# Scores of mixer A from rounded high and low parts of the keys, and a weight pool of 16 tiles of 4 KB

## The chip, the cores and the metric

The kernel runs on one core of a Trainium2 chip. The metric is the device time of one execution in microseconds, taken as the median of the runs. The engines are TensorE (PE in the profile, with its weight loads as PEld), VectorE (DVE), ScalarE (ACT), GpSimd (POOL) and SyncE (SP), which here issues every DMA. SBUF is the working memory of 128 partitions, PSUM the memory that matmuls write.

## The reference, cut to what matters

One layer of an encoder on 1024 prompt frames and 32 sample frames (1056 tokens of 1024 numbers, fp32): a SwiGLU feed-forward, a mixer of two attention kinds, a second feed-forward, each with norms and a modulation that a matrix w_mod makes from a conditioning vector. The change concerns mixer A, 8 heads of 64 with chunks of 64 frames:

```python
def band_attn_a(q, k, v, bias, valid):
    s = jnp.einsum('bnqhd,bnkhd->bnhqk', q, k).astype(jnp.float32) * SCALE + bias.astype(jnp.float32)
    s = jnp.where(valid[None, :, None], s, NEG_INF)
    p = jax.nn.softmax(s, axis=-1).astype(v.dtype)
    return jnp.einsum('bnhqk,bnkhd->bnqhd', p, v)
```

A frame reads its own chunk and the 8 chunks before it (576 keys). The keys of the last 512 frames are also an output (new_a_k_prompt). Mixer B is a window attention of 8 query heads and 2 key heads over 192 keys. All values are fp32, and the outputs must come out at near fp32 accuracy.

## The kernel before, in words

Tokens lie along the free dimension, in three blocks of 384, 384 and 288 (256 of the prompt and 32 of the sample). Every large product is made of rounded parts: a number is split into a rounded high part (type fp32r, written by an ACT copy) and the low rest (a DVE subtraction), and `mm3` (L278 to L281) adds high·high, high·low and low·high, three fp32r matmuls. Products whose operands are plain fp32 are one matmul in the code and two PE records in the trace.

**Stages.** The first feed-forward ends at about 918 us of the span, mixer B runs to about 1090, mixer A from 1094 to 1338, the output product and the second feed-forward after that.

**Mixer A.** Heads go in pairs p = 0 to 3 and queries in 8 tiles i of 128, so there are 32 tiles, each with two halves h (one head each). For tile i the band has L = 128, 256, 384, 512 and then four times 640 keys. A half is: the scores S (`qk`, L700), on PE; a bias on the last 256 columns (L710, DVE); a mask (L712, DVE, i at least 4); the row maximum (L714, DVE); the exponential with its sum (L717, ACT); a reciprocal (L718, DVE); the scaling, one in three on ACT (L720), the rest on DVE (L722); then the transposes of P (`tr`, L732, with copies out of PSUM at L659 and L661) and the product with the values (`av`, L669). Pairs 0 and 1 go one after the other, and between their pieces PE does the projections of the keys and queries of the next pairs (`pq`, three blocks per projection). Pairs 2 and 3 are interleaved, at which time there is no projection left; the group norms (`sq`, `z`, `o_hi`, `o_lo`) and the first pieces of the output product (`wo`) stand beside them.

**The score product.** A projection leaves keys and queries of a pair in one tile `KQ` (fp32, L933), keys of head 0 in partitions 0 to 63, of head 1 in 64 to 127. `pre` (L691) makes for each tile a stationary operand `qz` of 128 x 2 x 128 in which the other head's partitions are zero: two POOL memsets (L697) and two POOL copies (L698). The score is the plain fp32 product of that with all 128 partitions of the keys (L708), in pieces of up to 512 columns. Mixer B already works otherwise: its keys lie in `KSB` with the high part in partitions 0 to 63 and the low part in 64 to 127 (L1017, L1018), and its queries are split by `split_q` (L672) for each tile: DVE casts (L679), ACT copies the same to the other partitions (L677), DVE makes the low part (L680).

**Pools.** `wpool` has 8 tiles of 8 KB per partition, for split weights (high and low in one tile), for the raw w_mod pieces (two of 1 MB per column block), for V, KQ, the keys and queries of B, and for a tile `aux` of biases and cached V that two pairs share. `hpool` and `spool` have 5 tiles each. PSUM tiles `p1` (3 banks) serve gate, up, `pq`, `pp`, `wo`, and `p2` (2 of two banks) serve S and `dn`.

**Order.** The code is traced into a list; a scheduler with its own estimate of times then fixes each engine's order at build time and gives out the pool tiles as they come free. Each engine works its list strictly in that order.

Of the kernel before, what the change touches and what calls it, by code (L numbers as in the profile page):

```python
# [74 lines left out]
def encoder_step(ctx: ExitStack, tc, x_prompt, x_sample, cache_a_k, cache_a_v, cache_b_k, cache_b_v,  # L75
# [8 lines left out]
    wpool = ctx.enter_context(tc.tile_pool(name="wpool", bufs=8))  # L84
# [57 lines left out]
    jp = consts.tile([128, 128], I32, name="jp")  # L142
# [32 lines left out]
    def mod_chunk(n):  # L175
        raws = []
        for g in range(2):
            r = wpool.tile([128, 4, 512], F32, name="wm", tag="w")
            dma.dma_start(r, w_mod[0, 512 * g:512 * (g + 1), 512 * n:512 * (n + 1)]
                          .rearrange("(k p) n -> p k n", p=128))  # L180
            raws.append(r)
        bank = p1 if n < 4 else pc
        pm = bank("pm")
        for kk in range(2):
            for g in range(4):
                k = 2 * g + kk
                te.matmul(pm[32 * g:32 * g + 32, :], csil[:, k, :], raws[k // 4][:, k % 4, :],  # L187
                          start=kk == 0, stop=kk == 1)
# [78 lines left out]
    def split_vcols(wm, c0):  # L267
        out = []
        for h in range(2):
            r = rpool.tile([128, 4, 256], F32, name="raw", tag="r")  # L270
            dma.dma_start(r, wm[0, 512 * h:512 * h + 512, c0:c0 + 256].rearrange("(k p) n -> p k n", p=128))
            w = wpool.tile([128, 2, 4, 256], F32R, name="w", tag="w")
            ae.activation(w[:, 0], r, AF.Copy)
            ve.tensor_sub(w[:, 1], r, w[:, 0])
# [3 lines left out]
    def mm3(ps, w, k, hi, lo, start, stop):  # L278
        te.matmul(ps, w[:, 0, k], hi, start=start, stop=False)  # L279
        te.matmul(ps, w[:, 0, k], lo, start=False, stop=False)  # L280
        te.matmul(ps, w[:, 1, k], hi, start=False, stop=stop)  # L281
# [335 lines left out]
    def v_proj(ws, vt, vs):  # L617
        def piece(t, c0, n):
# [3 lines left out]
            for k in range(KT):  # L622
                wt, kk = ws[k // 4], k % 4
                a, b = hi[:, k, c0:c0 + n], lo[:, k, c0:c0 + n]
                te.matmul(ps[:n, :256], a, wt[:, 0, kk], start=k == 0, stop=False)
                te.matmul(ps[:n, :256], a, wt[:, 1, kk], start=False, stop=False)
                te.matmul(ps[:n, :256], b, wt[:, 0, kk], start=False, stop=k == KT - 1)
            o = vs if t == SEQ else vt[:, t // 128, :]
# [5 lines left out]
    def qk_proj(w, dst, dst_s, scale):  # L634
        def piece(tb):
# [7 lines left out]
            for a, b, st in SEGS[tb]:  # L643
                o = dst_s if st else dst[:, t0 + a:t0 + b]
# [37 lines left out]
    class TileA:  # L682
# [629 lines left out]
```

## Time and profile before

| | |
|---|---|
| median of 3 runs | 2239.25 us (2239.08 to 2243.16) |
| the profiled execution | 2243.16 us, span 2241.4 us |
| PE busy | 2179.2 us, 97% of the span |
| DVE, ACT, POOL busy | 1086.7, 703.7, 179.0 us |
| mean DMA share | 83 GB/s over the span |

A row of a group gives the line of the code, the engine, the operation, the tile written and the tiles read, the shape and the count; behind the bar the time that the group was busy, the mean of one in ns, and how long the engine sat idle just before such an instruction and for whom. In a table by stretches each engine has its busy time and, in brackets, its number of instructions; PEclk is the clock granted to TensorE as a share of full speed. Matmuls are pipelined: what one costs in a row of others is the step from one start to the next, and not its duration.

### The profile page before, as it was taken

How to read it: one execution, taken by the hardware profiler on the slowest of the kernel's cores; microseconds unless marked ns; L12 is line 12 of the kernel's file. 1: busy time of each engine (PE TensorE's matmuls, PEld its weight loads, DVE VectorE, ACT ScalarE, POOL GpSimd, SP SyncE). 2: the span in 40 equal slices, each digit the busy share in tenths (PEclk: the TensorE clock that was granted, in tenths of full speed). 3: DMA queues.
4: the chain of work that ended last, by engine and by line, in shares of the span. 5: the costliest groups of instructions: out<-in, count | busy, mean ns of one | idle time of the engine just before them, and what ended most of it. 6: DMA issues, size and time to landing. Idle time of an engine off the chain costs nothing.

```text
span 2241.4 us, 34009 instructions
## 1 busy us (share of the span) xinstructions
PE 2179.2 (97%) x14180; PEld 2063.9 (92%) x14180; DVE 1086.7 (48%) x2187; ACT 703.7 (31%) x1464; POOL 179.0 (8%) x281
## 2 busy tenths in 40 slices
PE   6999999999999999899999899999999999999998
PEld 4998999999999999889788579999999999999998
DVE  5733333332344387677544775776433333333336
ACT  4411101210121254476544673533211111111133
POOL 1100000000000022100100322310000000000000
PEclk9999999999999999899999899999999999999999
DMA  9256223422232244100211211422311111111122
GB/s 317 95 76 187 75 95 95 132 76 94 94 115 74 71 141 158 59 27 23 67 30 30 77 55 59 158 83 88 101 57 38 38 44 51 57 38 50 45 65 82
DMA packets 199901, 186.00 MB, mean 83 GB/s; under 512 B 6892, under 2 KB 169092, under 8 KB 198596
## 3 DMA queue, kind: packets, MB, share of 16 engines
q1 hardware_dynamic: 199748, 183.84, 26.9%
q8 instruction: 111, 1.82, 0.3%
q14 instruction: 42, 0.34, 0.1%
HBM read 160.98 MB, written 22.84 MB: 82 GB/s over the span
## 4 chain that ended last, share of the span: by engine, by line
PE 89%; DVE 5%; DMA 3%; ACT 2%; issue 1%; POOL 0%; SPq 0%; DVEq 0%; ACTq 0%; POOLq 0%
PE up L279 7%; PE up L281 7%; PE gate L279 7%; PE gate L281 7%; PE up L280 7%; PE gate L280 7%; PE dn L279 7%; PE dn L280 7%; PE dn L281 7%; PE po L669 2%; PE S L708 2%; PE pq L279 2%; PE pq L280 2%; PE pq L281 2%; PE pm L187 1%; PE wo L279 1%
## 5 line engine op out<-in xcount | busy, mean ns | idle before, releaser
L535 DVE TENSOR_TENSOR facc<-dn,facc 128x768 f32<-128x768 f32 (+1 forms) x240 | 213.1, 889 | 285.9 <-PE dn L281 285.8
L280 PE MATMUL gate<-h_lo,w 128*128 128x384 f32 (+1 forms) x1056 | 340.5, 322 | 4.0 <-DVE h_lo L400 4.0
L279 PE MATMUL up<-h_hi,w 128*128 128x384 f32 (+1 forms) x1056 | 341.2, 323 | 0.0
L279 PE MATMUL dn<-gg,w 128*128 128x384 f32 (+1 forms) x1056 | 339.8, 323 | 0.9 <-DVE facc L535 0.8
L279 PE MATMUL gate<-h_hi,w 128*128 128x384 f32 (+1 forms) x1056 | 340.6, 323 | 0.0
L280 PE MATMUL dn<-gg,w 128*128 128x384 f32 (+1 forms) x1056 | 339.6, 322 | 0.6 <-DVE gg L508 0.6
L281 PE MATMUL gate<-h_hi,w 128*128 128x384 f32 (+1 forms) x1056 | 340.2, 322 | 0.0
L280 PE MATMUL up<-h_lo,w 128*128 128x384 f32 (+1 forms) x1056 | 339.8, 322 | 0.0
L281 PE MATMUL up<-h_hi,w 128*128 128x384 f32 (+1 forms) x1056 | 339.4, 321 | 0.0
L281 PE MATMUL dn<-gg,w 128*128 128x384 f32 (+1 forms) x1056 | 339.4, 321 | 0.0
L258 DVE TENSOR_TENSOR w<-raw,w 128x1024 fp32r<-128x1024 f32 x187 | 231.6, 1246 | 143.4 <-ACT w L257 143.2
L505 DVE TENSOR_TENSOR sl<-sl,up 128x384 f32<-128x384 f32 (+1 forms) x132 | 68.6, 520 | 421.5 <-PE up L281 421.1
L257 ACT ACTIVATE w<-raw 128x1024 fp32r<-128x1024 f32 x187 | 195.8, 1056 | 244.2 <-PE dn L281 94.9
L504 ACT ACTIVATE sl<-gate 128x384 f32<-128x384 f32 (+1 forms) x132 | 61.0, 462 | 612.8 <-PE gate L281 612.7
L279 PEld LDWEIGHTS gate<-h_hi,w 128*128 128x128 f32 x1056 | 198.4, 188 | 5.9 <-ACT gg L507 5.0
L279 PEld LDWEIGHTS up<-h_hi,w 128*128 128x128 f32 x1056 | 198.4, 188 | 5.9 <-issue 5.9
L280 PEld LDWEIGHTS gate<-h_lo,w 128*128 128x128 f32 x1056 | 198.3, 188 | 4.7 <-DVE h_lo L400 4.7
L279 PEld LDWEIGHTS dn<-gg,w 128*128 128x128 f32 x1056 | 198.7, 189 | 1.6 <-DVE facc L535 1.2
L280 PEld LDWEIGHTS dn<-gg,w 128*128 128x128 f32 x1056 | 198.7, 188 | 1.0 <-DVE gg L508 0.9
L281 PEld LDWEIGHTS up<-h_hi,w 128*128 128x128 f32 x1056 | 198.7, 188 | 0.0
L281 PEld LDWEIGHTS dn<-gg,w 128*128 128x128 f32 x1056 | 198.6, 188 | 0.0
L280 PEld LDWEIGHTS up<-h_lo,w 128*128 128x128 f32 x1056 | 198.5, 188 | 0.0
(219 smaller groups left out, 3212.6 us busy)
## 6 DMA issues: line engine op xcount, KB each, us to landing
wm<-in_w_mod_dram SPq DMA_DIRECT2D x36, 1024.0 KB, 7.2
raw<-in_w_gate_dram SPq DMA_DIRECT2D x54, 512.0 KB, 4.7
raw<-in_w_up_dram SPq DMA_DIRECT2D x54, 512.0 KB, 35.1
raw<-in_w_down_dram SPq DMA_DIRECT2D x54, 512.0 KB, 4.6
raw<-in_w_in_dram SPq DMA_DIRECT2D x18, 512.0 KB, 3.9
raw<-in_w_out_dram SPq DMA_DIRECT2D x13, 512.0 KB, 3.6
xr<-xs SPq DMA_DIRECT2D x16, 384.0 KB, 5.0
raw<-xs SPq DMA_DIRECT2D x8, 512.0 KB, 4.5
```

The source lines that it names most:

```text
L187: te.matmul(pm[32 * g:32 * g + 32, :], csil[:, k, :], raws[k // 4][:, k % 4, :], start=kk == 0, stop=kk == 1)
L257: ae.activation(w[:, 0], r, AF.Copy)
L258: ve.tensor_sub(w[:, 1], r, w[:, 0])
L279: te.matmul(ps, w[:, 0, k], hi, start=start, stop=False)
L280: te.matmul(ps, w[:, 0, k], lo, start=False, stop=False)
L281: te.matmul(ps, w[:, 1, k], hi, start=False, stop=stop)
L504: ae.activation(sl[:, :w], ps[0][:, :w], AF.Silu)
L505: ve.tensor_tensor(sl[:, :w], sl[:, :w], ps[1][:, :w], op=OP.mult)
L535: ve.tensor_tensor(o, ps[:, :, :w], o, op=OP.add)
L669: te.matmul(po[64 * h:64 * h + 64, :n], vsl(j, h, kn), PT(h, j, kn), start=j == 0, stop=j == nt - 1)
L708: te.matmul(S[:, c:ce], self.T[:, h, :], KQ[:, 0, 128 * k0 + c:128 * k0 + ce], start=True, stop=True)
```

## The change

Keys and queries of mixer A are put in the form that mixer B has. A key projection no longer leaves fp32 keys: for each head a tile `KS` (fp32r) holds the rounded keys in the head's own 64 partitions (ACT) and the rest in the other 64 (DVE), for each of the three blocks. The query tile of `pre` gets four parts, by `split_q`: the rounded query in both halves of the partitions, and the low part over zeros. A score is then two fp32r products with the same keys: (high; high) with (key high; key low), and (low; 0). A band of 640 is taken as two pieces of 320 columns in two PSUM banks; the maximum and the exponential read both. Keys for the output are put together again by a product with `twice`, two identities on top of each other.

`wpool` becomes 16 tiles of 4 KB. High and low of a weight are two tiles, the w_mod pieces four of 512 KB, V and the keys of B two tiles each, and queries and `aux` have a tile for each pair. `qs` of mixer A is taken from `hpool`, where `qz` was in `spool`.

```diff
-    wpool = ctx.enter_context(tc.tile_pool(name="wpool", bufs=8))
+    wpool = ctx.enter_context(tc.tile_pool(name="wpool", bufs=16))
...
+    twice = consts.tile([128, 64], F32R, name="twice")
+    for h in range(2):
+        ae.activation(twice[64 * h:64 * h + 64], ident[64 * h:64 * h + 64, 64 * h:64 * h + 64], AF.Copy)
...
-        for g in range(2):
-            r = wpool.tile([128, 4, 512], F32, name="wm", tag="w")
+        for g in range(4):
+            r = wpool.tile([128, 2, 512], F32, name="wm", tag="w")
...
-        w = wpool.tile([128, 2, 8, 128], F32R, name="w", tag="w")
-        ae.activation(w[:, 0], r, AF.Copy)
-        ve.tensor_sub(w[:, 1], r, w[:, 0])
+        w = [wpool.tile([128, 8, 128], F32R, name="w", tag="w") for _ in range(2)]
+        ae.activation(w[0], r, AF.Copy)
+        ve.tensor_sub(w[1], r, w[0])
...
             for a, b, st in SEGS[tb]:
+                if put and not st:
+                    put(ps[:, a:b], slice(t0 + a, t0 + b))
+                    continue
...
         def pre(self):
-            T = self.T = s_tile([128, 2, 128], "qz")
-            cols = slice(128 * self.i, 128 * self.i + 128)
+            q = kqa[self.p]["q"][:, 128 * self.i:128 * self.i + 128]
+            T = self.T = h_tile([128, 4, 128], "qs", F32R)
             for h in range(2):
-                hp, op_ = slice(64 * h, 64 * h + 64), slice(64 - 64 * h, 128 - 64 * h)
-                ge.memset(T[op_, h, :], 0.0)
-                ge.tensor_copy(T[hp, h, :], kqa[self.p][0][hp, 1, cols])
+                ge.memset(T[64 - 64 * h:128 - 64 * h, 2 + h, :].bitcast(F32), 0.0)
+                split_q(T, h, q, T[64 * h:64 * h + 64, 2 + h, :])
...
-            for c in range(0, L, 512):
-                ce = min(L, c + 512)
-                te.matmul(S[:, c:ce], self.T[:, h, :],
-                          KQ[:, 0, 128 * k0 + c:128 * k0 + ce], start=True, stop=True)
+            m = (L + 511) // 512
+            S = p2("S")[:, :m, :L // m]
+            for c in range(m):
+                keys = K[:, 128 * k0 + c * L // m:128 * k0 + (c + 1) * L // m]
+                te.matmul(S[:, c], self.T[:, h, :], keys, start=True, stop=False)
+                te.matmul(S[:, c], self.T[:, 2 + h, :], keys, start=False, stop=True)
...
     def flow_ka(p, w):
-        KQ = wpool.tile([128, 2, 1024], F32, name="KQ", tag="w")
+        KS = [wpool.tile([128, 1024], F32R, name="KS", tag="w") for _ in range(2)]
+        def put(ps, cols):
+            for h in range(2):
+                hp, op = slice(64 * h, 64 * h + 64), slice(64 - 64 * h, 128 - 64 * h)
+                ae.activation(KS[h][hp, cols], ps[hp], AF.Copy)
+                ve.tensor_tensor(KS[h][op, cols], ps[hp], KS[h][hp, cols], op=OP.subtract)
...
         for j in range(4):
-            te.transpose(pk[:, j, :], KQ[:, 0, 512 + 128 * j:640 + 128 * j], ident)
+            for h in range(2):
+                te.matmul(pk[:, j, 64 * h:64 * h + 64], KS[h][:, 512 + 128 * j:640 + 128 * j], twice,
+                          start=True, stop=True)
```

The first place is PE near the end of mixer A, the last tile of pair 3 and the halves of scores that stand before the next piece of the output product (`pp` are transposes of P, `po` the product with V, `wo` the output product). Before:

```order
L732 MATMUL pp<-ident,P 128x128 x5
L669 MATMUL po<-PT,vt 64x128 x9
L708 MATMUL S<-KQ,qz 128x512
L708 MATMUL S<-KQ,qz 128x128
L708 MATMUL S<-KQ,qz 128x512
L708 MATMUL S<-KQ,qz 128x128
L732 MATMUL pp<-ident,P 128x128 x5
```

and with the change:

```order
L738 MATMUL pp<-ident,P 128x128 x5
L675 MATMUL po<-PT,vt 64x128 x10
L713 MATMUL S<-KS,qs 128x320
L714 MATMUL S<-KS,qs 128x320
L713 MATMUL S<-KS,qs 128x320
L714 MATMUL S<-KS,qs 128x320
L738 MATMUL pp<-ident,P 128x128 x4
```

A half of 640 keys was two instructions, of 512 and 128 columns, and is now four of 320. What stands around them is the same.

The second place is DVE in the stretch where pairs 2 and 3 are interleaved. Before:

```order
L710 TENSOR_TENSOR S<-S,aux 128x256
L718 RECIPROCAL den<-den 128x1
L712 MEMSET S 64x64
L722 TENSOR_SCALAR P<-P,den 128x640
L714 TENSOR_REDUCE nm<-S 128x1
```

and with the change:

```order
L685 CAST qs<-Q 64x128 x2
L716 TENSOR_TENSOR S<-S,aux 128x256
L686 TENSOR_TENSOR qs<-Q,qs 64x128 x2
L718 MEMSET S 64x64
L720 TENSOR_REDUCE nm<-S 128x1
L724 RECIPROCAL den<-den 128x1
L728 TENSOR_SCALAR P<-P,den 128x640
```

Four instructions of the query split (L685, L686), once for each tile, now stand in DVE's queue among the bias, mask and maximum of the scores; ACT has two more of them (L683), and POOL only the two memsets.

The third place is DVE where the keys of pair 3 (the tiles KS_11318 for head 0 and KS_11319 for head 1) come out of the three PSUM banks pq_11321, pq_11410 and pq_11488. Before, one ACT copy emptied each such bank. With the change:

```order
L946 TENSOR_TENSOR KS_11318<-pq_11321,KS_11318 64x384
L685 CAST qs_11434<-Q_10554 64x128 x2
L720 TENSOR_REDUCE nm_11398<-S_11394 128x1
...
L728 TENSOR_SCALAR P_11528<-P_11528,den_11527 128x640
L946 TENSOR_TENSOR KS_11319<-pq_11321,KS_11319 64x384
L946 TENSOR_TENSOR KS_11319<-pq_11410,KS_11319 64x384
L946 TENSOR_TENSOR KS_11318<-pq_11488,KS_11318 64x256
```

The parts of head 1 stand 20 rows behind the first part of head 0, so the banks pq_11321 and pq_11410 both stay taken until then.

More of the change, by code (lines that the diff above doesn't have):

```diff
@@ L271, in split_vcols @@
             dma.dma_start(r, wm[0, 512 * h:512 * h + 512, c0:c0 + 256].rearrange("(k p) n -> p k n", p=128))
-            w = wpool.tile([128, 2, 4, 256], F32R, name="w", tag="w")
-            ae.activation(w[:, 0], r, AF.Copy)
-            ve.tensor_sub(w[:, 1], r, w[:, 0])
+            w = [wpool.tile([128, 4, 256], F32R, name="w", tag="w") for _ in range(2)]
+            ae.activation(w[0], r, AF.Copy)
+            ve.tensor_sub(w[1], r, w[0])
             out.append(w)
@@ L905, in start_va @@
     def start_va(g, ws):
-        vt = wpool.tile([128, 8, 256], F32, name="vt", tag="w")
+        vt = [wpool.tile([128, 4, 256], F32, name="vt", tag="w") for _ in range(2)]
         vs = small.tile([32, 256], F32, name="vs", bufs=3)
@@ L940, in flow_qa @@
     def flow_qa(p, w):
-        KQ, KQs = kqa[p]
-        piece = qk_proj(w, KQ[:, 1, :], KQs[:, 1, :], 0.125)
+        Q = kqa[p]["q"] = wpool.tile([128, 1024], F32, name="Q", tag="w")
+        piece = qk_proj(w, Q, kqa[p]["s"][:, 1, :], 0.125)
         for tb in range(3):
@@ L967, in prepare @@
             return
-        if p % 2 == 0:
-            prep["aux"] = wpool.tile([128, 2, 2, 4, 128], F32, name="aux", tag="w")
-        aux = prep["aux"][:, p % 2]
+        aux = wpool.tile([128, 2, 4, 128], F32, name="aux", tag="w")
         cv = aux[:, 1]
@@ L988, in encoder_step @@
     wkv, wq0, wv0 = split_vcols(w_in, 2048), load_qb(0), load_va(0)
-    kvb = wpool.tile([128, 8, 256], F32, name="vt", tag="w")
+    kvb = [wpool.tile([128, 4, 256], F32, name="vt", tag="w") for _ in range(2)]
     kvbs = small.tile([32, 256], F32, name="vs", bufs=3)
@@ L1039, in encoder_step @@
         if tb == 2:
-            KSB = wpool.tile([128, 2, 1024], F32R, name="KSB", tag="w")
+            KSB = [wpool.tile([128, 1024], F32R, name="KSB", tag="w") for _ in range(2)]
             if PRIME:
```

66 lines of the change are left out of this document (32 added, 34 removed).

## The prediction

> **What bounds the kernel now.** I first read the engines' busy time on the page, then the busy time by stretches of mixer A, then the chain of waits there.
>
> ```profile
> PE 2179.2 (97%) x14180; PEld 2063.9 (92%) x14180; DVE 1086.7 (48%) x2187; ACT 703.7 (31%) x1464; POOL 179.0 (8%) x281
> ```
>
> Over the span PE is the bound and DVE is half idle. That average hides the stage that changes, so here it is cut: pairs 0 and 1 (with projections beside them), then three parts of pairs 2 and 3.
>
> ```profile
> 1095.00:1243.00 148.00, 144.38 (x975) 117.57 (x974) 68.14 (x167) 68.56 (x176) 16.29 (x64) 1.00 0.15 41
> 1243.00:1274.00 31.00, 25.83 (x156) 16.16 (x153) 25.49 (x71) 19.68 (x56) 14.84 (x33) 0.74 0.31 89
> 1274.00:1303.00 29.00, 27.19 (x174) 17.73 (x173) 22.71 (x77) 20.23 (x46) 8.74 (x21) 0.99 0.00 1
> 1303.00:1338.00 35.00, 34.29 (x235) 27.76 (x234) 26.59 (x53) 24.77 (x51) 6.50 (x8) 1.00 0.16 47
> ```
>
> The columns are PE, PEld, DVE, ACT, POOL, then the granted clock. In the first stretch PE is busy 144.4 of 148 us and DVE and ACT less than half: PE alone sets the time. In the next 95 us DVE is busy 25.49 + 22.71 + 26.59 = 74.8 us, 79%: both engines are near their limit there. The same stretches for the bias instruction, one for each half, give the tiles: 32 halves, then 12, 12 and 8.
>
> ```profile
> 1095.00:1243.00 148.00, 13.26 (x32) 1.00 0.15 41
> 1243.00:1274.00 31.00, 4.55 (x12) 0.74 0.31 89
> 1274.00:1303.00 29.00, 5.17 (x12) 0.99 0.00 1
> 1303.00:1338.00 35.00, 3.46 (x8) 1.00 0.16 47
> ```
>
> The chain of waits from 1090 to 1350 us says what the score product is worth there.
>
> ```profile
> by line: PE S L708 21.2%; PE po L669 13.8%; PE pq L279 10.0%; PE pp L732 9.5%; PE pq L280 9.1%; PE pq L281 9.1%; DMA ck<-in_cache_a_k_dram 3.0%; PE wo L280 2.8%; PE wo L281 2.7%; PE wo L279 2.6%; DVE z L1106 2.4%; issue 1.9%; ACT P L717 1.2
> 1110.02 0.43 PE S L708 x2
> 1115.67 0.65 PE S L708 x2
> 1120.37 0.86 PE S L708 x2
> 1151.33 1.08 PE S L708 x4
> ```
>
> L708 holds 21.2% of 260 us, 55 us: nearly all its work is on the chain. The pieces are one half each, of 256, 384, 512 and 640 keys.
>
> **The change part by part.** *Scores.* A half of 128 keys is 1.08 - 0.86 = 0.22 us. Eight halves of each small length and 32 of 640: 8 x (0.22 + 0.43 + 0.65 + 0.86) + 32 x 1.08 = 51.8 us. The new price is the step of fp32r matmuls in a row, from start to start:
>
> ```profile
> 1107.92 0.33 PE L280 MATMUL pq<-h_lo,w 128*128 128x384 f32 x1
> 1108.10 0.33 PE L281 MATMUL pq<-h_hi,w 128*128 128x384 f32 x1
> 1108.27 0.29 PE L279 MATMUL pq<-h_hi,w 128*128 128x288 f32 x1
> 1108.40 0.29 PE L280 MATMUL pq<-h_lo,w 128*128 128x288 f32 x1
> 1108.53 0.29 PE L281 MATMUL pq<-h_hi,w 128*128 128x288 f32 x1
> ```
>
> 384 columns take 0.17 us, 288 take 0.13. On that line 320 take 0.147, 512 take 0.23, 256 take 0.12; for 128 I take 0.11, as the old pieces of 128 had (0.22 / 2). Then the halves cost 4 x 0.147 = 0.59, 0.46, 0.34, 0.24 and 0.22: 8 x (0.22 + 0.24 + 0.34 + 0.46) + 32 x 0.59 = 29.0 us. PE loses 22.8 us of work, 11.4 in each half of the stage.
>
> *Keys for the output.* Four transposes (0.11 each, a 128-column piece) become eight products of 64 columns. They load 128 columns of weights as before, so at most 0.11 each, at least 0.055 by columns: 0 to +0.44 us for each pair; I take the upper end, since the small pieces above go by their weights. Three fall in the first stretch: +1.3.
>
> *DVE, ACT and POOL.* Mixer B has the new instructions:
>
> ```profile
> L677 ACT ACTIVATE qs<-qbt x64: 307/308/312, 916.8 to 1080.1; 64x128 fp32r<-64x128 f32 x64
> L679 DVE CAST qs<-qbt x64: 197/224/646, 920.5 to 1078.8; 64x128 fp32r<-64x128 f32 x64
> L680 DVE TENSOR_TENSOR qs<-qbt,qs x64: 262/285/716, 923.7 to 1079.5; 64x128 fp32r<-64x128 f32 x64
> L698 POOL COPY qz<-KQ x64: 283/288/1869, 1075.0 to 1306.3; 64x128 f32<-64x128 f32 x64
> L1018 DVE TENSOR_TENSOR KSB<-pk,KSB x4: 684/690/698, 929.2 to 940.3; 64x512 fp32r<-64x512 f32 x4
> L710 DVE TENSOR_TENSOR S<-S,aux x64: 272/433/433, 1095.1 to 1337.5; 128x256 f32<-128x256 f32 x56, 128x128 f32<-128x128 f32 x8
> L645 ACT ACTIVATE KQ<-pq x24: 375/486/494, 1055.8 to 1228.3; 128x384 f32<-128x384 f32 x16, 128x256 f32<-128x256 f32 x8
> ```
>
> For each tile DVE gets 2 x (0.224 + 0.285) = 1.02 us, ACT 2 x 0.308 = 0.62; POOL loses 2 x 0.288. For each key projection DVE gets two subtractions of 384, 384 and 256 columns: between 0.433 (256) and 0.690 (512) the 384 are 0.56, so 2 x (0.56 + 0.56 + 0.43) = 3.1 us; ACT copies each block twice instead of once, 2 x 0.486 + 0.375 = 1.35 more. In all DVE +32 x 1.02 + 4 x 3.1 = 45 us.
>
> *First stretch.* PE loses 11.4 - 1.3 = 10.1 us. DVE goes to 68.1 + 16 x 1.02 + 3 x 3.1 = 93.7 of some 138 us (68%), ACT to 68.6 + 9.9 + 4.1 = 82.6 (60%). Mixer B bears more than that with PE never idle:
>
> ```profile
> 960.00:1000.00 40.00, 40.00 (x303) 35.99 (x302) 31.71 (x109) 28.24 (x100) 2.77 (x9) 1.00 0.12 34
> ```
>
> DVE is at 79% there and PE at 100%, so the gain should arrive. Against it stands the third place of the order: a bank of a key projection stays taken through two copies and two subtractions, which wait in DVE's queue, and behind them PE's next `pq` or `pp` needs one of three banks. Bounds: nothing, where PE has other work; and for pair 3, 20 rows of DVE at about 0.4 us (68.14 / 167), 8 us, less the pieces that PE has in front (24 `pq` at 0.13, 8 scores at 0.147, five `po`: 5 us), 3 us. I take 1: the stretch gives **-9 us**.
>
> *Last 95 us.* PE loses 11.4 us, DVE gets 16 x 1.02 = 16.3, over 6, 6 and 4 tiles: 31.6, 28.8 and 30.7 us, 91.1 in all. What DVE can be filled to is the unknown. The chain leaves it these holes:
>
> ```profile
> DVE S L710 <- PE S L708: 10.5, 15, 1.8
> DVE den L718 <- ACT P L717: 3.4, 5, 0.9
> 1310.00:1320.00 10.00, 9.29 (x61) 7.44 (x60) 8.88 (x18) 6.30 (x15) 1.25 (x1) 1.00 0.00 1
> ```
>
> 10.5 of its 20 idle us are waits for scores, which now come in half the time, and nobody waits at once for a query split, which is made a tile ahead; so it can fill holes. The best 10 us seen are 89% full. At 100% the stretch takes 91 us (-4); at 83%, little over what it has, 110 (+15). I take 92%, over the best seen for the two reasons: 99 us, **+4 us**.
>
> *The pool of 16 tiles.* The bytes are the same. Pairs 2 and 3 now hold 10 of 16 tiles (keys 4, queries 2, `aux` 2, V 2) where they held 4 of 8, so three instead of four weights of the output product fit beside; each stays for one piece of PE work, so I take nothing, and if its cover is gone a wait of one split (1.2 us on DVE). At the start four more DMAs go ahead of the first weight.
>
> ```profile
> 7.52 0.37 SPq L179
> 7.93 0.51 SPq L179
> 8.49 12.11 DMA raw<-in_w_gate_dram
> ```
>
> At up to 0.51 us each that is 2 us of issue, and it lies in front of a transfer of 12 us that queues behind the same bytes: 0 to +2, I take 0. The two copies that make `twice` run before the first input has landed: nothing.
>
> [...] In the second row PE's clock is 0.74 of full speed while PE is busy 25.83 of 31 us. [...]
>
> Sum: -9 + 4 = -5. On the profiled 2243.16 us that gives 2238; that execution is the highest of the three, so on the median of 2239.25 I predict **2234 us**.
>
> **The rivals.** *DVE becomes the bound* (slower). Place: DVE's queue from 1243 to 1338. If it fills to no more than 83%, the stretch costs +15, and with -9 the time is 2245. It decides from 84% down (91.1 / 0.84 = 108.5, +13.5 - 9 = +4.5). For it: 79% now, and ACT waits on the row maximum behind DVE's queue. Against: the holes above. *The whole gain arrives*: DVE fills every hole, -9 - 4 = -13: 2226. For it: L708 on the chain; against: no row shows DVE at 100%. *The first stretch is eaten*: banks of keys and late weights stop PE for 6 of its 10 us, and with +4 nothing is left: 2239. Against: PE at 100% beside a DVE at 79%. [...]
>
> **How the numbers follow.** This forecast has 0.38, its own range 2230 to 2238; the whole gain 0.17; the first stretch eaten 0.16; the gate 0.07; DVE as the bound 0.22. A measurement of this kernel tells 0.2%, 4.5 us, from no change, so faster means below 2234.8: 0.25 of the forecast and the whole gain, 0.42. The other 0.13, with the eaten stretch and the gate, is no change: 0.36. Slower is 0.22. For 8 in 10 the range leaves out the far ends of the first two rivals: 2224 to 2247.
>
> **What would show it.** Right: halves of 640 at 0.6 us in the chain; the first stretch some 9 us shorter with PE still over 95%; the last one 95 to 102 us with DVE above 88% and PE with holes. Wrong: waits of `pq` or `pp` for L946's banks in the first stretch; DVE under 85% in a longer last one; a clock under 0.8 after 1274; or a difference that lies outside mixer A, since every order was made anew.

## The result, and the profile after

The change made the kernel slower: 2260.07 us (median; 2257.07 to 2261.9) against 2241.2 us (2239.08 to 2244.28) for the kernel before on the same chip, a ratio of 1.0086 with a 95% interval of 1.0067 to 1.0104. The forecast was 2234 us with a range up to 2247, so it missed on the wrong side. The profiled execution took 2259.58 us with a span of 2257.7, that is 16.3 us more than the span before.

The first row of the page after the change:

```profile
PE 2176.0 (96%) x14196; PEld 2073.5 (92%) x14196; DVE 1131.7 (50%) x2339; ACT 730.1 (32%) x1542; POOL 162.5 (7%) x217
```

DVE has 45.0 us more and ACT 26.4: the sums of the prediction (45, and 32 x 0.62 + 4 x 1.35 = 25). That DVE's sum agrees is in part chance: the rows of the query and key splits alone add up to 49.7 us, as some took longer than priced. PE's busy time hardly moved, and that alone says little, since a matmul at the lower clock is busy for longer: from 1105 to 1115 us, where the granted clock is 0.64 and 0.67, a `pq` matmul of 384 columns takes 0.52 us, and 0.33 right behind. So here are the stretches of mixer A that the prediction cut, after the change. The columns are again length, PE, PEld, DVE, ACT, POOL, granted clock, DMA share, GB/s.

```profile
1102.00:1250.00 148.00, 142.50 (x1023) 123.39 (x1020) 93.94 (x255) 84.13 (x218) 6.24 (x30) 0.98 0.20 52
1250.00:1285.00 35.00, 25.13 (x146) 17.40 (x146) 32.25 (x96) 23.79 (x71) 10.49 (x19) 0.64 0.19 55
1285.00:1316.00 31.00, 26.24 (x181) 20.59 (x181) 27.84 (x96) 21.33 (x51) 5.24 (x13) 0.85 0.01 1
1316.00:1354.00 38.00, 36.23 (x257) 31.38 (x257) 34.11 (x70) 30.69 (x62) 7.72 (x11) 1.00 0.28 83
```

Below, the *first stretch* is from the first bias of pair 0 to the first bias of pair 2, the *last stretch* from there to the last bias. The bias instruction gives both ends:

```profile
L716 DVE TENSOR_TENSOR S<-S,aux x64: 271/433/433, 1102.7 to 1354.0; 128x256 f32<-128x256 f32 x56, 128x128 f32<-128x128 f32 x8
```

Mixer A begins at 1102.7 instead of 1095.1 (+7.6). Its first stretch is no shorter (148 us as before, where 139 were forecast), and its last stretch took 104 us instead of 95 (99 were forecast): 94.2 us of DVE work, 91% full, with the clock at 0.64 and 0.85 in its first two parts where it had been 0.74 and 0.99. The last bias is 16.5 us late, and so is the end. So there are three losses to explain: 7.6 us ahead of mixer A, a gain of 9 that did not come, and 5 us more than forecast at the end.

The scores themselves got as cheap as forecast. A half of 640 keys in PE's order of time (start, length, engine and line):

```profile
1218.62 0.41 PE L713 MATMUL S<-KS,qs 128*128 128x320 f32 x1
1218.87 0.31 PE L714 MATMUL S<-KS,qs 128*128 128x320 f32 x1
1219.02 0.31 PE L713 MATMUL S<-KS,qs 128*128 128x320 f32 x1
1219.16 0.31 PE L714 MATMUL S<-KS,qs 128*128 128x320 f32 x1
1219.31 0.27 PE L738 MATMUL pp<-ident,P 128*128 128x128 f32 x1
```

From start to start the later pieces take 0.14 to 0.15 us (0.147 forecast), the half 0.69 with 0.1 more on its first piece (0.59 forecast, 1.08 before). Adding up for all 192 pieces the time from a piece's start to the next start on PE, or to its own end if that is earlier, gives 61.1 us before and 40.8 after: 20 of the 22.8 us are really gone from PE.

The same sum over the whole span tells what stands in their place. PE is idle for 69.7 us after the change and for 50.3 before; the products for the key output take 1.7 us more; and all other matmuls, of which there are as many as before, take 15 us more (the largest parts: `po` 3.7, `pp` 3.0, `pq` and `pv` 2.1 each, `pm` 1.9), at a mean granted clock of 0.980 instead of 0.988. So the spared time became idle time, and slower matmuls came on top. The question is what made them.

### The profile page after: what moved, and what is told of

Same layout as the page of the kernel before. It is cut to its first block, busy times and chain, and to the rows that moved or that the text cites. A ratio compares the mean times of both kernels' runs of the same rounds, so it can differ in the third digit from the quotient of the medians.

```text
span 2257.7 us, 34387 instructions
## 1 busy us (share of the span) xinstructions
PE 2176.0 (96%) x14196; PEld 2073.5 (92%) x14196; DVE 1131.7 (50%) x2339; ACT 730.1 (32%) x1542; POOL 162.5 (7%) x217
## 5 line engine op out<-in xcount | busy, mean ns | idle before, releaser
L282 PEld LDWEIGHTS gate<-h_hi,w 128*128 128x128 f32 x1056 | 198.8, 188 | 11.0 <-ACT gg L510 5.0
L284 PEld LDWEIGHTS gate<-h_hi,w 128*128 128x128 f32 x1056 | 198.9, 188 | 0.0
```

Of the source, the lines that this page charges most:

```text
L282: te.matmul(ps, w[0][:, k], hi, start=start, stop=False)
L284: te.matmul(ps, w[1][:, k], hi, start=False, stop=stop)
```

## The experiments

Each kernel was timed beside the kernel before on one chip. All compute the whole reference; three of them do some work more, as said there. The table has the ratio to the kernel before, and from the bias rows of the profiled execution the shift of mixer A's start against the kernel before (1095.1) and the lengths of the two stretches (before: 148.5 and 93.9 us).

| kernel | median us | ratio, 95% interval | start of mixer A | first stretch | last stretch |
|---|---|---|---|---|---|
| the change | 2260.07 | 1.0086 (1.0067 to 1.0104) | +7.6 | 147.7 | 103.6 |
| new tiles, old scores | 2250.09 | 1.0043 (1.0030 to 1.0056) | +7.1 | 147.4 | 98.2 |
| before, smaller transfers at the start | 2244.93 | 1.0029 (1.0017 to 1.0041) | +4.7 | 148.2 | 88.6 |
| new tiles, new scores in pairs 0, 1 | 2248.27 | 1.0040 (1.0028 to 1.0053) | +8.5 | 142.8 | 92.1 |
| new tiles, new scores in pairs 2, 3 | 2265.09 | 1.0121 (1.0107 to 1.0135) | +10.6 | 150.8 | 102.6 |
| change, query split on GpSimd | 2251.94 | 1.0052 (1.0040 to 1.0065) | +9.4 | 147.1 | 94.2 |
| change, subtraction twice | 2275.97 | 1.0162 (1.0146 to 1.0178) | +5.5 | 148.4 | 119.5 |
| change, PE kept busy | 2262.00 | 1.0104 (1.0091 to 1.0117) | +7.0 | 147.6 | 103.5 |
| change, scaling on ScalarE | 2257.21 | 1.0072 (1.0060 to 1.0084) | +4.8 | 147.9 | 93.8 |
| change, GpSimd split and scaling on ScalarE | 2254.05 | 1.0057 (1.0041 to 1.0073) | +6.3 | 147.3 | 98.7 |
| old tiles, new scores in pairs 0, 1 | 2234.63 | 0.9975 (0.9965 to 0.9985) | 0.0 | 144.6 | 93.0 |
| old tiles, new scores in pair 0 | 2236.13 | 0.9980 (0.9971 to 0.9989) | +2.2 | 143.5 | 91.8 |
| the same as two rows up, PE kept busy at the start | 2237.85 | 0.9989 (0.9979 to 0.9999) | +2.6 | 141.8 | 92.7 |

A stretch of one execution is good to a few us and no better: the fp32 scores alone, in the same place, stand here with 88.6 to 98.2 us in the last stretch, as the order differs. Nor do the borders cut off the same work everywhere. In the change, and in the rows of the new tiles with old scores, pairs 2 and 3, the query split, the double subtraction, PE kept busy, and GpSimd split with scaling on ScalarE, 96 matmuls of the output product (`wo`) lie in the last stretch; in all others, the kernel before with them, 72 or 73. The 24 more are worth 4 us (17.2 against 13.2 us from start to start, with fp32 scores in both). And behind the last bias the kernels take between 900.2 and 910.4 us, so a shorter stretch is not always a shorter kernel.

**The tiles alone.** The change with its 16 tiles and the old scores:

```
-        KS = [wpool.tile([128, 1024], F32R, name="KS", tag="w") for _ in range(2)]
+        K = wpool.tile([128, 1024], F32, name="K", tag="w")
...
-                te.matmul(S[:, c], self.T[:, h, :], keys, start=True, stop=False)
-                te.matmul(S[:, c], self.T[:, 2 + h, :], keys, start=False, stop=True)
+                te.matmul(S[:, c:ce], self.T[:, h, :],
+                          K[:, 128 * k0 + c:128 * k0 + ce], start=True, stop=True)
```

> The kernel before with the 16 tiles of 4 KB and everything that they changed (four transfers for each block of the modulation weights, values, keys, queries and bias in halves), but the scores as they were: fp32 keys, one product, no split of mixer A's queries or keys. Theory 1, what arose ahead of mixer A (7.6 us of span until its first score) and between pairs 1 and 2 (5.3 us) is the pool's and the order's that came with it: the span grows by 5 to 13 us on the kernel before, with the first score of mixer A 5 to 8 us later and the last stretch (pairs 2 and 3) as before. Rival, all of it comes from the scores and only shows elsewhere: within 3 us of the kernel before.

Measured: +10.1 us on the kernel before, as theory 1 had it, and over half of what the change costs, though not a single score differs from it. Its bias row and its two stretches:

```profile
L713 DVE TENSOR_TENSOR S<-S,aux x64: 272/433/433, 1102.2 to 1347.8; 128x256 f32<-128x256 f32 x56, 128x128 f32<-128x128 f32 x8
```

```profile
1102.00:1249.00 147.00, 143.77 (x976) 117.31 (x974) 67.97 (x168) 69.31 (x176) 18.07 (x64) 1.00 0.16 45
1249.00:1348.00 99.00, 92.41 (x615) 67.28 (x609) 78.81 (x204) 69.35 (x159) 33.15 (x64) 0.91 0.19 55
```

Mixer A starts 7.1 us late, as in the change: that loss belongs to the tiles. The last stretch is 4 us longer as well, against the expectation. That is its border: 24 more `wo` matmuls and two more weight splits of the output product fall into it (DVE does 78.81 us there instead of 74.8), and 2.9 us come back behind it. The 5.3 us that the expectation sought between pairs 1 and 2 are not here: they belong to the scores.

**Only the transfers at the start.** The kernel before, with two lines changed:

```
-            dma.dma_start(r, w_mod[0, 512 * g:512 * (g + 1), 512 * n:512 * (n + 1)]
-                          .rearrange("(k p) n -> p k n", p=128))
+            for a in (0, 2): dma.dma_start(r[:, a:a + 2], w_mod[0, 512 * g + 128 * a:512 * g + 128 * a + 256,
+                          512 * n:512 * (n + 1)].rearrange("(k p) n -> p k n", p=128))
```

> The kernel before with each 1 MB transfer of the modulation weights made as two of 0.5 MB into the halves of the same tile; nothing else. Theory 1a, the number of transfers at the start makes the 4 to 5 us that arose before 300 us: 2243 to 2246 us, with the same steps at 70 and 200 us. Rival, the smaller tiles make them (weights and halves are handed on apart, in another order): within 2 us of the kernel before.

Measured: +5.1 us, as expected, and mixer A starts 4.7 us late. In size that is half of what the tiles cost. But it does not come as the expectation had it, at the same places. Among the waits of PE in the first 260 us, these are long in this kernel, and the next two in the change (what waits, for what; total, times, longest). The kernel before waits 3.8 us in four for `wm` and 1.5 us for `xt`, and has neither of the waits for `gg` and `sl`.

```profile
PE pm L187 <- DMA wm<-in_w_mod_dram: 3.7, 2, 3.4
PE pt L571 <- ACT xt L573: 3.7, 1, 3.7
PE dn L280 <- DVE gg L508: 3.3, 1, 3.3
```

```profile
PE gate L282 <- DVE sl L508: 2.9, 1, 2.9
PE pm L190 <- DMA wm<-in_w_mod_dram: 2.4, 4, 1.5
```

Neither list has its long waits where the other has. What the two have in common is that the instructions of the first FFN were put in another order. Nor is it the sum of the waits that this kernel loses: up to the same place in the first FFN (300 us in the kernel before) PE is idle for 14.8 us, against 15.1 before. The same matmuls take longer there, `gate` by 1.2 us, `dn` and `pt` by 1.8 each, and the clock is lower; from 45 to 110 us, in the kernel before and then in this one:

```profile
45.00:110.00 65.00, 62.01 (x393) 60.83 (x391) 49.08 (x107) 32.32 (x63) 13.03 (x14) 1.00 0.39 134
45.00:110.00 65.00, 60.22 (x348) 58.69 (x348) 48.89 (x106) 32.99 (x64) 13.67 (x14) 0.93 0.40 134
```

The change has 1.7 us more of idle time up to that place, and its products with w_mod (`pm`) take 1.9 us more. So more transfers alone can cost as much, but that the change pays for the same thing is not shown. With the tiles alone PE is 4.0 us late from 250 us on and 6.9 in mixer B; which of the split tiles brings the later part was not separated.

**Half of the pairs each.** New tiles in both; `NEWP` says which pairs get the new scores, keys and query split.

```
+NEWP = (0, 1)      # and (2, 3) in the other
...
+            if self.p not in NEWP:
+                return self.qk_old(h)
```

> The 16 tiles of 4 KB throughout; pairs 0 and 1 have the rounded two-product scores, pairs 2 and 3 the fp32 scores of the kernel before. Against the kernel with the new tiles and old scores (2250 us, 10 over the kernel before). Theory 3, in pairs 0 and 1 PE is the bound and most of its saved work arrives: 4 to 8 us under that kernel, 2242 to 2246 us. Rival, the saved PE work is lost at once at the start of mixer A and in the key banks: within 2 us of 2250.

> The other half: pairs 0 and 1 with fp32 scores, pairs 2 and 3 with the rounded two-product scores, the 16 tiles of 4 KB throughout. Theory 2, VectorE's 16 us more in pairs 2 and 3 outweigh what PE is spared: 5 to 10 us over the kernel with the new tiles and old scores, 2255 to 2260 us. Rival, the loss comes from the first pairs or from all four together: within 3 us of 2250.

Measured, in us over the kernel before: old scores 10.1, pairs 0 and 1 new 8.4, pairs 2 and 3 new 25.3, all four 18.9. The new scores are worth about -2 in pairs 0 and 1 and +15 in pairs 2 and 3; the two effects don't add up exactly (13 against 9), and every order is another. The -2 is not clear of noise (the intervals of the two kernels overlap), so by its time it is the rival that held in pairs 0 and 1; the +15 is more than the 5 to 10 expected. The stretches, of pairs 0 and 1 new and then of pairs 2 and 3 new:

```profile
1103.00:1246.00 143.00, 138.07 (x994) 120.83 (x990) 84.49 (x236) 78.39 (x207) 8.59 (x41) 0.98 0.19 52
1246.00:1339.00 93.00, 85.39 (x557) 60.57 (x556) 74.20 (x200) 65.06 (x150) 29.81 (x64) 0.93 0.20 58
```

```profile
1105.00:1256.00 151.00, 147.88 (x1014) 120.37 (x1011) 76.76 (x188) 74.47 (x186) 15.24 (x52) 1.00 0.17 47
1256.00:1359.00 103.00, 86.44 (x582) 68.30 (x581) 94.11 (x260) 75.51 (x184) 23.13 (x42) 0.85 0.18 51
```

In the first stretch the new scores of pairs 0 and 1 save 4.6 us (147.4 to 142.8), half of the forecast. Little of it reaches the end: against the tiles alone the last stretch is 6.1 us shorter, 4 of them since 24 `wo` matmuls fewer lie in it, and what stands behind it is 9.4 us longer. Pairs 2 and 3, whose keys are projected and split in the first stretch, make it 3.4 us longer (147.4 to 150.8). Of these, 2.0 are work that now falls ahead of the border (19 more matmuls of `po`, 5 of `pps`) and 0.8 the products for the key output; PE is idle no longer than with the tiles alone (3.3 against 3.2 us). In the change, where both come together, the stretch is as long as with the tiles alone.

The last stretch with new scores in pairs 2 and 3 is 4.4 us longer than with the tiles alone (102.6 against 98.2, 96 `wo` in both), with DVE at 94 of 103 us, where the prediction's second term has it. The rest of the 15 us stands elsewhere: 3.5 ahead of mixer A, 3.4 in the first stretch, 6.3 behind the last one, in an execution that is 4.5 us over its kernel's median.

**VectorE's work in the last stretch, less and more.** The split of mixer A's queries with its rounded copy and its subtraction on GpSimd; and the change with each subtraction done twice:

```
-                split_q(T, h, q, T[64 * h:64 * h + 64, 2 + h, :])
+                split_q(T, h, q, T[64 * h:64 * h + 64, 2 + h, :], "gag")
```

```
                 split_q(T, h, q, T[64 * h:64 * h + 64, 2 + h, :])
+                ve.tensor_tensor(T[64 * h:64 * h + 64, 2 + h, :], q[64 * h:64 * h + 64],
+                                 T[64 * h:64 * h + 64, h, :], op=OP.subtract)
```

> The change with mixer A's query split taken off VectorE: the rounded copy of the first part and the subtraction are on GpSimd, the second copy stays on ScalarE. VectorE loses 16 x 1.0 us in pairs 2 and 3. Theory 2, VectorE's fill sets the length of the last stretch (104 us, 94 of them VectorE's work): at the same 91% the work of 78 us takes 86, so the stretch comes down to PE's bound of some 90 us, and the time to 2243 to 2250 us. Rival, the stretch is long because a score bank is handed on late or PE's clock is low whatever VectorE has to do: within 4 us of the change, or longer since GpSimd's subtraction is slower and a tile's queries come late.

> The change with each query subtraction of mixer A done twice on VectorE, 64 more instructions of 0.29 us and nothing else: 18.4 us of VectorE, half of it in pairs 2 and 3. Theory 2, VectorE's fill sets the last stretch and not the first: 8 to 11 us more in pairs 2 and 3, under 2 us more in pairs 0 and 1, 2267 to 2272 us. Rival, VectorE still has holes to fill: under 4 us more in all.

Measured: 8 us less and 16 us more than the change, the way that theory 2 has it, though 2251.94 us is just over the range expected and 2275.97 above it. GpSimd's subtraction takes 0.452 us (median, in the last stretch), where VectorE's takes 0.289 in the change. The last stretches, with GpSimd's split and with the doubled subtraction, whose first stretch stands ahead of it:

```profile
1251.00:1346.00 95.00, 82.74 (x581) 66.53 (x579) 77.41 (x201) 74.48 (x184) 47.01 (x98) 0.89 0.19 55
```

```profile
1100.00:1249.00 149.00, 143.54 (x1042) 124.29 (x1038) 103.55 (x289) 84.83 (x222) 6.13 (x30) 0.98 0.20 54
1249.00:1369.00 120.00, 95.63 (x564) 75.36 (x561) 103.73 (x287) 75.27 (x180) 22.57 (x43) 0.77 0.14 40
```

The first stretch takes 9.6 us more of DVE work without a change (149 with the boundaries rounded); the last one pays 16 for 9.5. So in the last stretch VectorE's work is on the path, and more than one to one: DVE is only 86% full in the 120 us, and its waits in them are about as long for PE (4.8 us), whose clock is at 0.77, as for ScalarE (5.9). And the other way: with DVE at 77 us the stretch falls from 103.6 to 94.2 (86 were expected). With fp32 scores and the same tiles and `wo` matmuls it took 98.2, so 4 of the 10 us spared on PE show there; 2.3 of them come back behind it, and the whole time is no better than with fp32 scores (1.0052 against 1.0043).

**Is it the clock?** In the change, two matmuls more ahead of each score half of pairs 2 and 3, into a bank that nothing reads:

```
+            if p >= 2:
+                warm = pc("warm")
+                for _ in range(2):
+                    te.matmul(warm[:64], twice, K[:, 0:512], start=True, stop=True)
```

> The change with two matmuls more ahead of each score half of pairs 2 and 3, 64 in all, 64x512 into the eighth PSUM bank, which nothing reads: 0.23 us each at full clock, 15 us of PE work that keeps it busy while it waits for a score bank. Theory 4, the lower granted clock in the last stretch (0.64 and 0.85) costs time of its own, as the po and pp rows run slower there: with PE busier the clock stays higher, and the time is the same or up to 5 us shorter, 2254 to 2261 us. Rival, theory 2 alone (VectorE sets the time, the clock only follows): the extra work partly fills holes, 0 to 5 us longer, or up to 15 where PE is the bound.

Measured: 2262.0 us, and the last stretch took 103.5 us (103.6 in the change). The whole stretch, and its first part:

```profile
1249.00:1353.00 104.00, 93.22 (x625) 71.83 (x623) 90.69 (x255) 74.72 (x182) 22.84 (x42) 0.90 0.16 46
1249.00:1284.00 35.00, 29.26 (x165) 18.58 (x165) 30.11 (x96) 24.37 (x72) 9.86 (x19) 0.76 0.20 60
```

PE's score and transpose matmuls in that stretch, with the extra work and then in the change (busy, mean ns | idle before):

```profile
L742 PE MATMUL pp<-ident,P 128*128 128x128 f32 x105 | 19.0, 298 | 1.1 <-ACT PT L667 0.5 <-DVE P L732 0.4
L717 PE MATMUL S<-KS,qs 128*128 128x320 f32 (+4 forms) x47 | 17.7, 386 | 6.0 <-ACT P L727 3.6 <-DVE S L720 0.8 <-ACT qs L683 0.7
```

```profile
L738 PE MATMUL pp<-ident,P 128*128 128x128 f32 x105 | 20.3, 320 | 2.8 <-DVE P L728 1.4 <-DVE rv L348 0.7 <-ACT PT L667 0.5
L713 PE MATMUL S<-KS,qs 128*128 128x320 f32 (+4 forms) x47 | 19.8, 431 | 9.0 <-ACT P L723 6.0 <-DVE S L716 1.8 <-DVE qs L685 0.7
```

The clock rose from 0.84 over the stretch to 0.90, the same matmuls got shorter, and PE did some 20 us of work that serves nothing (62 of the 64 matmuls lie in the stretch, 0.33 us each from start to start) without the stretch getting any longer. So the rise of the clock bought nothing there, as the rival has it: in these two runs the lower clock comes with the longer holes, 9.0 us ahead of the first pieces of the scores at 0.84 and 6.0 at 0.90. How far this settles the question of the clock has its limits: the clock in the first part is still 0.76, 20 `po` matmuls fewer lie in the stretch (220 against 240), and behind it come 3.2 us more than in the change.

**More relief for VectorE.** Two of three probability tiles scaled on ScalarE (`SC = (1, 3)` to `SC = (2, 3)`), in the change and together with GpSimd's split:

> The change with the scaling of two of three probability tiles on ScalarE instead of one of three: in pairs 2 and 3 some ten instructions of 0.55 us leave VectorE. Theory 2, VectorE sets the last stretch: 4 to 7 us less there, 2253 to 2256 us. Rival, ScalarE (77% busy there) is then as full and its row maximum and exponent come late: within 3 us of 2260, or over it.

> The change with both reliefs of VectorE at once: rounded copy and subtraction of mixer A's queries on GpSimd, and two of three probability tiles scaled on ScalarE. Theory 2, with VectorE near 70% in pairs 2 and 3 the spared PE work shows there: the last stretch falls from 94 us (GpSimd's split alone) to under 92, the time to 2245 to 2250 us, still over the kernel before by the small tiles' cost. Rival, with VectorE spared ScalarE (89.6 of 120 us with GpSimd's split) or GpSimd is what ends last: no less than 2252 us.

Measured: 3 us under the change by the ratios, with intervals that overlap, where 4 to 7 were expected; and no less than GpSimd's split alone (1.0057 against 1.0052). The last stretch of the one and of the other:

```profile
1247.00:1342.00 95.00, 79.46 (x538) 63.01 (x538) 86.56 (x244) 76.42 (x186) 22.06 (x41) 0.84 0.15 44
```

```profile
1248.00:1348.00 100.00, 87.71 (x582) 70.00 (x579) 73.79 (x192) 81.40 (x198) 45.69 (x99) 0.85 0.19 53
```

The first is from an execution 5 us under its kernel's median and has 24 `wo` matmuls fewer, so its 95 us don't compare with the others. The second has DVE at 74% and is longer than with DVE at 81% (one execution of each): by that VectorE no longer sets the time there, and the rival holds. What does then is not settled. PE is at 88 of 100 us at a clock of 0.85, ACT at 81, and every tile passes from PE to DVE to ACT and back through two score banks.

**Only where PE is the bound, in the old tiles.** The kernel before, with the new scores in pairs 0 and 1 alone, then in pair 0 alone. Queries get a tile of their own, both parts of the keys one.

```
+NEWP = (0, 1)      # (0,) in the other
...
+        KS = wpool.tile([128, 2, 1024], F32R, name="KS", tag="w") if p in NEWP else wpool.tile([128, 2, 1024], F32, name="KQ", tag="w")
```

> The kernel before with its 8 tiles of 8 KB and two transfers for each block of the modulation weights; pairs 0 and 1 alone have the rounded two-product scores (the two key parts of a pair in one tile, the queries of both pairs in one tile more), pairs 2 and 3 the fp32 scores. If the small tiles cost 10 us, the rounded scores in pairs 2 and 3 12 to 15, and in pairs 0 and 1 are worth 2 to 9: 2231 to 2238 us, with mixer A starting as in the kernel before and 5 to 9 us gained by the first score of pair 2. Rival, the tile more that the queries hold makes weights late and eats it, or the order made anew costs as much as with the small tiles: 2240 to 2250 us.

> As the run beside it, with pair 0 alone in the rounded form. Theory 3, PE's saved work of 5.7 us a pair arrives in proportion: half of what that run gains, 2235 to 2239 us. Rival, the gain is order and not work: no more or no less than that run, or nothing.

Measured: 2234.63 and 2236.13 us, ratios 0.9975 and 0.9980, both faster than the kernel before and within the ranges expected, and the first some 25 us faster than the change. Mixer A of the first starts where it did before, its first stretch is 3.9 us shorter (5 to 9 were expected) and its last one no longer. Pair 0 alone gains about as much (the intervals overlap, and its first stretch is no longer), so the gain does not go by the work spared: theory 3 falls in its simple form, and of pair 1's 5 us almost nothing arrives.

Where the first stretch loses can be seen at its start, in two slices of 5 us of the kernel before and then of this one, each with PE's wait for a score bank from 1090 to 1105 us, and for the second kernel the one for `o` ahead of it, which is 1.3 us in the kernel before:

```profile
1095.00:1100.00 5.00, 3.43 (x26) 2.62 (x26) 4.94 (x13) 4.24 (x12) 3.27 (x8) 1.00 0.70 199
1100.00:1105.00 5.00, 5.00 (x45) 4.67 (x44) 1.20 (x6) 1.45 (x5) 0.05 (x1) 1.00 0.13 39
```

```profile
PE S L708 <- ACT Ps L844: 1.3, 1, 1.3
```

```profile
1095.00:1100.00 5.00, 2.60 (x19) 1.86 (x15) 4.36 (x12) 4.02 (x11) 0.00 (x0) 0.72 0.66 171
1100.00:1105.00 5.00, 5.00 (x19) 5.00 (x19) 2.92 (x11) 1.59 (x7) 0.00 (x0) 0.59 0.28 83
```

```profile
PE S L718 <- ACT Ps L889: 2.2, 1, 2.2
PE po L676 <- ACT o L668: 2.1, 1, 2.1
```

PE waits 2.2 us for a score bank instead of 1.3, the clock falls to 0.59, and 19 matmuls pass in 5 us where 45 passed before. The change has the same at its place, behind waits of 1.4 us (for `qs` of DVE), 0.8 (for a score bank) and 1.0 (for `Ps` of DVE):

```profile
1105.00:1110.00 5.00, 3.27 (x18) 2.49 (x15) 4.75 (x13) 3.76 (x12) 0.00 (x0) 0.64 0.84 219
1110.00:1115.00 5.00, 5.00 (x33) 4.75 (x33) 1.70 (x8) 0.95 (x5) 0.00 (x0) 0.67 0.00 0
```

A dozen `pq` matmuls of 384 columns pass there at 0.32 us from start to start instead of 0.17. Over the first stretch the same 432 `pq` matmuls take 75.1 us in the change and in this kernel, 73.4 in the kernel before, and 73.5 with new scores in pairs 2 and 3 alone, where the clock stays at 1.00 at the start of mixer A.

**The hole at the start of mixer A.** To that kernel, four matmuls ahead of each score half of the first two tiles, into a bank that nothing reads:

```
+            if p == 0 and i < 2:
+                warm = pc("warm")
+                for _ in range(4):
+                    te.matmul(warm[:64], twice, K[:, 0:512], start=True, stop=True)
```

> The kernel with 8 tiles of 8 KB and rounded scores in pairs 0 and 1 (2234.6 us), with four 64x512 matmuls of the key parts ahead of each score half of the first two tiles of mixer A, 16 in all, into the eighth PSUM bank, which nothing reads: 0.23 us each. There PE waits 2.2 us for a score bank and its granted clock falls to 0.72 and 0.59 for 10 us (1.00 in the kernel before). Theory 5, the longer hole shuts the gate and that is where part of the saved work in pairs 0 and 1 goes: with the hole partly filled the clock stays over 0.9 in those 10 us and the first score of pair 2 comes 1 to 3 us earlier, 2232 to 2234 us. Rival, the clock stays low or the extra work only delays the scores: 0 to 4 us longer.

```profile
1095.00:1100.00 5.00, 4.62 (x32) 2.49 (x30) 4.14 (x10) 3.59 (x10) 0.00 (x0) 1.00 0.92 255
1100.00:1105.00 5.00, 5.00 (x32) 4.24 (x31) 4.83 (x18) 3.25 (x10) 0.00 (x0) 1.00 0.47 139
```

The clock stays at 1.00, the 432 `pq` matmuls take 73.1 us, and the first stretch falls by 2.8 us more, to 141.8. By the `pq` matmuls the low clock had cost 2 us of that. The whole time is not better for it, though (0.9989 against 0.9975, the intervals overlap; 2232 to 2234 us were expected): mixer A starts 2.6 us later in this order. So the mechanism is shown in its stretch and no use of it in the total.

New scores in all four pairs with the old tiles have no time: that kernel ends in a deadlock before it can run. Expected were 2238 to 2247 us if the tiles cost what arises outside mixer A's tiles, and 2255 to 2262 if the scores do; so what the scores of pairs 2 and 3 cost is known in the new tiles alone. The likely cause, not shown, is that with two tiles' worth of key parts for each pair and the queries beside them, the pairs in flight hold more tiles than the eight there are.

## Why the prediction was wrong, step by step

*The price of the scores: right.* 0.15 us a piece; 20 of 22.8 us are gone from PE. The keys for the output cost what the upper end said: their matmuls take 1.7 us more over all pairs, as one of 64 columns takes 0.112 us from start to start and a transpose of 128 columns took 0.109.

*The first stretch, -9 forecast, -0.8 measured: the step that failed first.* The scores did leave PE: added up as above, they take 17.0 us there instead of 27.2. What failed is the step from there to the time: that a PE spared 10 us ends the stretch 9 us earlier, because it was busy 144.4 of 148 us. About 4 us are filled by work that now falls ahead of the border, which the forecast left where it was (22 `po`, 5 `pps` and 2 `ppb` matmuls more); 1.3 are the products for the key output, as forecast; 2.3 are the same `pq` and `pp` matmuls, slower; and PE is idle for 2.1 us more. The last two belong for the most part to the stretch's start, where the first tiles have no cover: there the new chain (query split, then score, then a bank held through maximum and exponent) made the holes longer and the clock fell, to 0.64 and 0.67 in the change, where it was 1.00 before. The 1 us that the prediction took for the key banks can't be found: the waits of PE in this stretch after the change list one `pq` wait of 0.2 us and none of `pp` for L946.

*The last stretch, +4 forecast, +9.7 measured: right mechanism, a term too small.* Of the 9.7 us, 4.3 stand already in the run with the tiles alone, where the 24 more `wo` matmuls are; the scores add 5.4. Its fill was taken as 92% and came out as 91%. Its work was taken as 91.1 us and came out as 94.2. Two groups of it are larger than forecast, here in the change from 1250 to 1354 us:

```profile
L686 DVE TENSOR_TENSOR qs<-Q,qs 64x128 fp32r<-64x128 f32 x30 | 13.1, 438 | 0.6
L261 DVE TENSOR_TENSOR w<-raw,w 128x1024 fp32r<-128x1024 f32 x10 | 12.2, 1219 | 1.6 <-ACT w L260 1.5
```

The subtraction took 438 ns and not the 285 of mixer B (+4.6 us), and ten weight splits fall in the stretch instead of eight (+2.4 us, and the tiles alone show it too). Against them, the query split of one tile and the sample's scores, 1 us each, are done before it. The holes that the prediction meant DVE to fill were filled, its waits for the scores went from 10.5 us to

```profile
DVE S L716 <- PE S L714: 1.9, 4, 0.7
```

So PE's spared 10 us count for nothing in this stretch as long as VectorE is full, and for little when it isn't: with VectorE relieved to 77 us it takes 94.2 against 98.2 with fp32 scores in the same tiles. PE was at 92% there, but as a waiter among others.

*The pool of 16 tiles, 0, and the start, 0 with bounds of 0 and +2: wrong, +10.1 us in the median.* The prediction priced the transfers by their issue time and the tiles by their bytes, and put both at nothing. With the tiles alone, mixer A starts 7.1 us late. More transfers alone, in the old tiles, make a new order that costs 5.1 us with no more idle time; for the change itself it stays open which part of the tiles costs what. No row of the profile before showed a price for a new order. The prediction did name this among what would prove it wrong, a difference outside mixer A, and gave it no chance and no room in the range.

*The rivals.* VectorE as the bound: right in place, at 91% instead of the 83% it asked for. The first stretch eaten: right, by other means. They were set against each other as cases, and both came true at once. The gate, given 0.07: no run shows a gate, only the granted clock beside the waits. A lower one had no cost of its own that could be seen in the last stretch, within the limits said. At the start of mixer A, where the prediction did not look, it cost some 2 us: the `pq` matmuls of the first stretch take 75.1 us in the change and 73.4 in the kernel before, and with new scores in pairs 0 and 1 in the old tiles 75.1, or 73.1 with PE kept busy. The waits quoted above are of 2.1 and 2.2 us ahead of a clock of 0.72 and 0.59, with work between them; ahead of the change's 0.64 and 0.67 none is over 1.4.

With the measured terms in place of its own the sum is 7.6 ahead of mixer A, -0.8 and +9.7 inside it, -0.2 behind it: +16.3 us, the difference of the spans.

## What to carry to other kernels

Cost an edit in the stretch where it acts, and split it by stretch if the bound differs: here the same scores gain up to 5 us in the pairs where PE is the bound and cost 15 in those where the vector engine is full, and the version that takes only the first half, in the old tiles, beats both kernels. When a change needs other buffer sizes or other transfers, measure those alone first; here they cost as much as the change proper. When a stretch's length is compared, count the work that its borders cut off: 24 matmuls on the other side of one are 4 us here. And a PE at 97% can still have a place without cover, where a hole one microsecond longer is paid twice, by the wait and by the clock: here 2.2 us instead of 1.3 for a score bank, and a clock of 0.72 and 0.59 instead of 1.00.

## What was not expected of the hardware

The subtraction's 438 ns are not an even slowing. Most take 0.29 us, and some take 1.05: those that run while GpSimd squares the group norm's inputs (`sq`, 128x384). VectorE and GpSimd after the change, from 1300 us (start, length):

```profile
1300.77 1.29 DVE L685 CAST qs<-Q 64x128 fp32r<-64x128 f32 x2
1302.09 0.43 DVE L716 TENSOR_TENSOR S<-S,aux 128x256 f32<-128x256 f32 x1
1302.56 1.60 DVE L686 TENSOR_TENSOR qs<-Q,qs 64x128 fp32r<-64x128 f32 x2
```

```profile
1300.73 1.00 POOL L325 TENSOR_TENSOR sq<-sq 128x384 f32<-128x384 f32 x1
1301.94 0.99 POOL L325 TENSOR_TENSOR sq<-sq 128x384 f32<-128x384 f32 x1 [0.21 <-ACT sq L321]
1303.01 1.00 POOL L327 TENSOR_TENSOR sq<-sq 128x384 f32<-128x384 f32 x1
```

Two copies take 1.29 us instead of 0.43, two subtractions 1.60 instead of 0.58, and each slow one ends with or just behind a squaring; the bias between them, which works on PSUM, keeps its 0.43. All eight copies and subtractions of mixer A's queries over 0.4 us overlap such an instruction; two more overlap one and keep their time, and both of these had begun before it. Against the usual 0.22 us of a copy and 0.29 of a subtraction, such a meeting costs up to 0.8 us. So the price read in a stretch with little GpSimd work (mixer B's 285 ns, with GpSimd busy for 2.77 of 40 us in the prediction's row) was too low for this one, where GpSimd is busy for 23.45 of 104 us.
